# A hybrid attention step: token scales applied to x at the start, the second norm applied to the result, ReLU on ScalarE

## The chip, the cores and the metric

The kernel runs on one NeuronCore of a Trainium2 chip. The core has a matrix engine (TensorE, PE in the profile), VectorE (DVE), ScalarE (ACT), GpSimd (POOL) and SyncE (SP); here SP issues every DMA. Each engine works through its own list of instructions in order and waits at an instruction until what it needs is there. The metric is the device time of one execution in microseconds (us).

## The reference

One layer for 512 prompt tokens and 64 sample tokens (8 sequences of 8), model width 1024, all in fp32. The outputs are y for all 576 tokens, the new keys and values, and the states of the delta rule and of the convolution. What matters here:

```python
hn = rmsnorm(x, norm1_g)
proj = hn @ w_in
# mixer A: gated delta rule on qkv_a (short conv, l2norm), 4 heads of 128
oa = rmsnorm(oa, delta_norm_g) * silu(z_a)
# mixer B: dilated softmax attention, 8 heads of 64
qb = rmsnorm(q_b, q_norm_g); kb = rmsnorm(k_b, k_norm_g)
ob = dilated_attention(qb, k_all, v_all, k_past.shape[1])
h1 = x + concatenate([oa, ob]) @ w_o
hid = square(relu(rmsnorm(h1, norm2_g) @ w_up))
y = h1 + hid @ w_down
# rmsnorm(x, g) = x * rsqrt(mean(x * x) + 1e-6) * g
```

In an rmsnorm the factor of a token is one number for its whole row. It can therefore be applied before or after a product with a weight matrix, and for the squared ReLU as its square behind the MLP.

## The kernel before

**Order.** The program writes the instruction list of every engine at build time. A planner, `Flow` (lines 91 to 209), runs the pieces of the program as tasks: each task yields instructions, and the planner always takes the one that could start first by its table of costs and latencies, plus a bias by kind of task (`fl.biases`, line 1912: a task with a large bias goes behind the others). Tasks of kind "fill" are the large projections, which go where no other work for TensorE is due. The order is fixed once it is written; on the chip each engine keeps it, whatever the real durations are. Tiles come from pools with a number of slots for each use (`klass`, line 335 and on): `"q"` has 8 slots of 128x576, `"big"` 6, `"g"` (PSUM for the projections) up to 8. A task that finds no free slot stops until one is released.

**Precision.** An fp32 matrix product is three matmuls in the chip's fp32r form: high by high, high by low, low by high. So each operand is split first: ScalarE makes the high part, VectorE the rest (`wh`, `wl` for weights; `mw` holds both parts in the MLP; `xh`, `xl` for x; `xf` for the factors of the MLP's input). One matmul of a 128x128 weight block with 288 tokens is the unit of work.

**Stages.** Tokens lie along the free axis (576 of them, two halves of 288), features on partitions.

- x is loaded into `xr`, multiplied by the norm's gain g1 and split. Its mean square by token, `var1`, is taken from ScalarE's squares, GpSimd's adds and a column sum on TensorE (`ssum`). The first norm itself isn't applied to x; the stages that need it correct for it.
- proj_a (tile `pa`) makes q, k, v of the attention from the weights wq, wk, wv. proj_b (`pg<-xh`, `pg<-xl`) makes the columns of the delta mixer from wb.
- Prompt attention (`sc` scores, `e` exponentials, `ptp` their transposes, `pv`) and sample attention (`s` scores, `os` output) are laid between the matmuls of proj_b. Sample attention reads the cache in 48 loads of 512 KB, through slots `kv` and, once prompt attention has given up its memory, four more, `morekv`.
- The delta mixer: a substitution with a trip through HBM (`dl`, `dU`, loads `silvz`), triangular levels (`py`, `pt`, `pu`), and then the chain over four heads with four chunks of 128 tokens each (`cha`, `chb`; 44 matmuls in `cha`). Its sample part is `cs` and `sn`. `head_out` norms the output (`vo`, `po`).
- proj_o multiplies by w_o, first the attention half (`pg<-mob`, 192 matmuls) and then the delta half (`pg<-moa`). The first may begin when both attentions are through, and is fill beside the chain. `after_o` adds the products to the residual `h`, which `load_res` had loaded from the input.
- The MLP: z = h * g2 * S goes into quads of tiles `xq`, one quad for two feature tiles, four quads. S is a scale by token, (var1 + 1)^-1/2, taken up in `token_scale`. Two units of 128 hidden features by two (u0 and u1, "classical") use z's four parts; units u2 to u15 use a Strassen-like scheme of seven products, which also needs sums of the parts, the T sums (`t_sums`). Units of the down projection (`d`) follow. The second norm's factor R2 is known only when the squares of h are summed over all features (`square_sum`, `stats2`); it is laid out along tokens by `row_bcast` (matmuls `rowb`, copies on ScalarE).

**What the change touches.** In `x_factors` a quad takes four "q" tiles; two hold the parts of z and two the T sums. Four quads would need 16 slots, and there are 8. ReLU and R2 are applied in one VectorE pass out of PSUM, so no hidden unit can go on before R2 is there:

```python
        z = hx[i].q[2 * hf + m % 2]
        act(z, x, scale=C["g2"][:, m:m + 1])
        yield 0
        tt(z, z, st2["S"][:, c0:c1], OP.mult)
...
        yield lambda: "R2b" in done
        c0, c1 = HALF[hf]
        stt(Q[u].q[2 * hf + r], P, 0.0, st2["S"][:, c0:c1], OP.max, OP.mult)
```

Of the kernel before, what the change touches and what calls it, by code (L numbers as in the profile page):

```python
# [10 lines left out]
F32 = mybir.dt.float32  # L11
# [201 lines left out]
def hymba_step(ctx: ExitStack, tc: tile.TileContext, a):  # L213
# [106 lines left out]
    def dma(dst, src, mark=None, slow=1):  # L320
# [17 lines left out]
                      "mr": 2, "ms": 2, "mw": 6})  # L338
# [228 lines left out]

    def prep_x():
# [24 lines left out]
        rel("x", "st", "st", "big")  # L593
# [5 lines left out]
        sig("rbc")  # L599

# [172 lines left out]
    def prompt_attn():  # L773
        yield lambda: all((w, t) in done for w in "qkv" for t in range(4))
# [8 lines left out]
    def unit(u):  # L783
# [28 lines left out]
        for h in range(2):  # L812
            ts(e[h], e[h], sm[:, h, 2:3], None, OP.mult)
# [55 lines left out]
    def sample_unit(bp, qbd, sbt, sbn):  # L869
# [51 lines left out]
        ts(sm[:, 5:9], C["msel"], sm[:, 4:5], None, OP.mult)  # L921
# [230 lines left out]
    def dap(t, ap_, off=0):  # L1152
        return bass.AP(tensor=t.tensor, offset=t.offset + off, ap=ap_)

# [120 lines left out]
    def head_tokens(h):  # L1275
# [38 lines left out]
        ts(tq[:, h], ssq[:, h], 128 * EPS, 512 * EPS * EPS, OP.mult, OP.add)  # L1314
        sig(("tq", h))
# [231 lines left out]
    def head_out(c):  # L1547
# [5 lines left out]
        stt(v[:n], sso[:n, c], 1.0 / DA, tq[:n, :, c], OP.mult, OP.add)  # L1553
# [32 lines left out]
    def after_delta():  # L1586
# [4 lines left out]
        st2["acc"] = yield from get("k", [128, NT], "acc2")  # L1591
        st2["sq"] = yield from get("k", [128, 864], "sq2")
# [8 lines left out]
    def load_res():  # L1601
        yield lambda: "kv" in done
        for m in range(KT):
            x = yield from get("h1", [128, NT], "h1")
            dma(x, a["xT"][:, m], lambda t, m=m: rest.update({m: t}))
            h1[m] = x
            sig(("res", m))
            yield 0

    def after_o(m, hf, p, last):  # L1610
# [15 lines left out]
        yield 0  # L1626
        tt(z, z, st2["S"][:, c0:c1], OP.mult)
# [4 lines left out]
    def square_sum(m, hf):  # L1632
# [3 lines left out]
        if m:  # L1636
            n = 2 * m + hf
            last = [("sq", m - 1, hf)] + [("sq", (n - 3) // 2, (n - 3) % 2)] * (n >= 5)
            if not all(x in done for x in last):
                yield lambda: all(x in done for x in last)  # L1640
            n = n % 3 * 288
            s = st2["sq"][:, n:n + 288]
# [8 lines left out]
    OF_X = {1: 0, 2: 1, 3: 3, 4: 7, 5: 4, 6: 5, 7: 6}  # L1651
# [3 lines left out]
    class Quad:  # L1655
        def __init__(self, tiles):
            self.t = tiles
            self.q = [blk(tiles[j // 2], j % 2) for j in range(8)]
# [4 lines left out]
    def quad(name):  # L1663
        t = []
        for j in range(4):
# [7 lines left out]
    def t_sums(x, key):  # L1673

        q = x.q
        tt(q[4], q[2], q[0], OP.subtract)
        yield 0
        tt(q[5], q[3], q[4], OP.subtract)
        yield 0
        fl.spawn(x_parts(x, key, 4, 2), "tsum")  # L1680
        tt(q[6], q[3], q[2], OP.subtract)
        yield 0
        tt(q[7], q[1], q[5], OP.subtract)
        yield 0
        fl.spawn(x_parts(x, key, 6, 2), "tsum")
# [355 lines left out]
```

## Time and profile before

| | |
|---|---|
| median of three timed runs | 818.09 us (817.8 to 819.38) |
| the profiled execution: its own time, its span | 818.95 us, 817.2 us |
| busy in the span: TensorE, VectorE, ScalarE, GpSimd | 792.2, 568.7, 348.3, 109.4 us |
| the same as shares | 97%, 70%, 43%, 13% |
| mean DMA rate | 121 GB/s |

The profile is of one execution. Its time is 1.75 us longer than its span, which runs from the first to the last instruction. A share over the whole span hides the stages; the rows further down take it by stage. In a timeline, "[3.08 <-ACT xf L270]" says that the engine stood idle for 3.08 us before this row and that ScalarE's instruction on tile xf ended the wait.

### The profile page before, as it was taken

How to read it: one execution, taken by the hardware profiler on the slowest of the kernel's cores; microseconds unless marked ns; L12 is line 12 of the kernel's file. 1: busy time of each engine (PE TensorE's matmuls, PEld its weight loads, DVE VectorE, ACT ScalarE, POOL GpSimd, SP SyncE). 2: the span in 40 equal slices, each digit the busy share in tenths (PEclk: the TensorE clock that was granted, in tenths of full speed). 3: DMA queues.
4: the chain of work that ended last, by engine and by line, in shares of the span. 5: the costliest groups of instructions: out<-in, count | busy, mean ns of one | idle time of the engine just before them, and what ended most of it. 6: DMA issues, size and time to landing. Idle time of an engine off the chain costs nothing.

```text
span 817.2 us, 15699 instructions
## 1 busy us (share of the span) xinstructions
PE 792.2 (97%) x6323; PEld 728.1 (89%) x6323; DVE 568.7 (70%) x1250; ACT 348.3 (43%) x728; POOL 109.4 (13%) x128
## 2 busy tenths in 40 slices
PE   8989998999999999999997999999999999999998
PEld 8968877879778687778997999999999999999998
DVE  4366269888776785668798886768677676867642
ACT  5547453655242134443466543515343351534400
POOL 3443224134224000121000000000000000000000
PEclk9999999999999999999999999999999999999999
DMA  7732320106686799122221141404123130412302
GB/s 270 125 112 77 123 68 31 55 27 245 211 345 185 273 319 327 49 93 81 104 104 52 59 150 52 129 27 155 53 94 113 52 129 27 155 53 95 112 30 87
DMA packets 49864, 99.05 MB, mean 121 GB/s; under 512 B 12864, under 2 KB 26304, under 8 KB 49792
## 3 DMA queue, kind: packets, MB, share of 16 engines
q1 hardware_dynamic: 49792, 98.05, 36.6%
q8 instruction: 50, 0.82, 0.4%
q14 instruction: 22, 0.18, 0.1%
HBM read 88.15 MB, written 9.69 MB: 120 GB/s over the span
## 4 chain that ended last, share of the span: by engine, by line
PE 73%; issue 9%; DVE 7%; DMA 6%; ACT 2%; SPq 2%; POOL 1%; POOLq 0%; ACTq 0%; DVEq 0%
PE pg L262 53%; PE pa L262 7%; DVE y L285 2%; SPq L321 2%; PE cha L262 2%; DMA wr<-in_wk_dram 2%; DMA morekv<-in_cv_dram 1%; PE os L262 1%; PE ptp L265 1%; DMA morekv<-in_ck_dram 1%; PE cs L262 1%; DMA silvz<-dU 1%; PE sc L262 1%; PE s L262 1%; PE sn L262 1%
## 5 line engine op out<-in xcount | busy, mean ns | idle before, releaser
L262 PE MATMUL pg<-hid,mw 128*128 128x288 f32 x1536 | 204.7, 295 | 0.0
L262 PEld LDWEIGHTS pg<-hid,mw 128*128 128x128 f32 x1536 | 203.9, 188 | 0.0
L262 PE MATMUL pg<-xf,mw 128*128 128x288 f32 x1368 | 186.0, 297 | 4.6 <-ACT xf L270 3.8
L262 PEld LDWEIGHTS pg<-xf,mw 128*128 128x128 f32 x1368 | 183.7, 189 | 5.6 <-ACT xf L270 4.3
L278 DVE TENSOR_TENSOR h<-pg,h 128x288 f32<-128x288 f32 x160 | 72.5, 455 | 94.6 <-PE pg L262 93.8
L270 ACT ACTIVATE mw<-wr 128x512 fp32r<-128x512 f32 (+1 forms) x82 | 62.9, 791 | 70.8 <-PE pg L262 70.1
L262 PE MATMUL pg<-xh,wh 128*128 128x288 f32 x256 | 78.0, 305 | 0.0
L262 PE MATMUL pg<-xl,wh 128*128 128x288 f32 x256 | 78.0, 305 | 0.0
L262 PE MATMUL pg<-xh,wl 128*128 128x288 f32 x256 | 77.9, 304 | 0.0
L278 DVE TENSOR_TENSOR mw<-wr,mw 128x512 fp32r<-128x512 f32 (+1 forms) x82 | 72.4, 893 | 6.7 <-ACT mw L270 6.3
L270 ACT ACTIVATE mw<-ws 128x512 fp32r<-128x512 f32 x56 | 33.7, 627 | 45.3 <-PE pg L262 26.6
L262 PEld LDWEIGHTS pg<-xh,wh 128*128 128x128 f32 x256 | 48.4, 189 | 3.2 <-issue 3.0
L262 PEld LDWEIGHTS pg<-xh,wl 128*128 128x128 f32 x256 | 48.4, 189 | 2.8 <-issue 2.4
L262 PEld LDWEIGHTS pg<-xl,wh 128*128 128x128 f32 x256 | 48.5, 189 | 2.5 <-issue 1.9
L308 POOL TENSOR_TENSOR wl<-wr,wh 128x1024 fp32r<-128x1024 f32 x15 | 35.9, 2393 | 81.6 <-ACT wh L270 65.0
L262 PE MATMUL pa<-wh,xh 128*128 128x260 f32 (+1 forms) x128 | 43.1, 344 | 1.0 <-ACT wh L270 1.0
L262 PE MATMUL pa<-wh,xl 128*128 128x260 f32 (+1 forms) x128 | 43.6, 348 | 0.5 <-DVE xl L285 0.4
L262 PE MATMUL pa<-wl,xh 128*128 128x260 f32 (+1 forms) x128 | 42.7, 341 | 0.0
L270 ACT ACTIVATE wh<-wr 128x1024 fp32r<-128x1024 f32 (+1 forms) x40 | 38.6, 964 | 8.0 <-DMA wr<-in_wk_dram 5.1
L270 ACT ACTIVATE uq<-pg 128x288 f32<-128x288 f32 x42 | 17.1, 408 | 58.0 <-PE pg L262 58.0
L285 DVE SCALAR_TENSOR_TENSOR y<-u,cp,y 128x600 f32<-128x600 f32 x36 | 37.1, 1032 | 5.9 <-ACT u L270 3.3
L278 DVE TENSOR_TENSOR wl<-wr,wh 128x1024 fp32r<-128x1024 f32 (+1 forms) x25 | 28.4, 1134 | 16.0 <-ACT wh L270 15.9
(295 smaller groups left out, 1311.1 us busy)
## 6 DMA issues: line engine op xcount, KB each, us to landing
wr<-in_wu_dram SPq DMA_DIRECT2D x32, 512.0 KB, 3.3
wr<-in_wd_dram SPq DMA_DIRECT2D x32, 512.0 KB, 3.3
morekv<-in_ck_dram SPq DMA_DIRECT2D x20, 512.0 KB, 5.4
morekv<-in_cv_dram SPq DMA_DIRECT2D x20, 512.0 KB, 5.3
wr<-in_wb_dram SPq DMA_DIRECT2D x16, 512.0 KB, 4.0
wr<-in_wo_dram SPq DMA_DIRECT2D x8, 512.0 KB, 6.1
xr<-in_xT_dram SPq DMA_DIRECT2D x8, 288.0 KB, 5.6
h<-in_xT_dram SPq DMA_DIRECT2D x8, 288.0 KB, 7.2
```

The costliest lines, as they stand in the source:

```text
L262: lambda: nc.tensor.matmul(out, lhsT, rhs, start=start, stop=stop, skip_group_check=True))
L265: fl.op("PE", (97, 230), lambda: nc.tensor.transpose(out, in_, ident[:k, :k]))
L270: fl.op("ACT", cost, lambda: nc.scalar.activation(out, in_, func, bias=bias, scale=scale, accum_out=accum), mark)
L278: dve(lambda: nc.vector.tensor_tensor(out, x, y, op=op), out, x, mark=mark)
L285: dve(lambda: nc.vector.scalar_tensor_tensor(out, x, s, y, op0=op0, op1=op1), out, x, 61 if ap(s) else 0, mark=mark)
L308: fl.op("POOL", (135 + size(x) / 0.47) * slow, lambda: nc.gpsimd.tensor_tensor(out, x, y, op=op), mark)
L321: fl.op("SP", 4 * slow * size(dst) * dst.shape[0] / 360.0, lambda: nc.sync.dma_start(dst, src), mark)
```

## The change

- `scales` and `scale_x` are new: right after var1 the scale S is computed (`sc1`), laid out along tokens, and x is multiplied by it on VectorE (eight passes of 128x576). The scaled x is stored in HBM (`xsd`, eight stores), and `load_res` loads the residual from there. S also goes through HBM into `ssc`, in the layout of sample attention (one store, 16 loads). Prompt attention may begin when these loads are issued.
- Attention takes S up where e is normalised; `head_out` takes it up through `vp` and `vpa`. So all of h is scaled, and z needs no multiply by S.
- A quad takes two "q" tiles. The T sums are made in place, once the first four parts of all four quads are split.
- The second norm leaves the hidden units: ReLU is a ScalarE pass. When the token sums are there, h is multiplied by isc * R2 (`scale_h`, eight passes of 128x576), and the result by 1 / R2 just before it is stored (16 passes of 128x288). For the wait between, PSUM has 7 instead of 8 slots for "g" until R2 is laid out.
- The biases of the T sums and of the token sums (kind "acc") change, and the classical unit is written by output block.

```diff
-                      "mr": 2, "ms": 2, "mw": 6})
+                      "mr": 2, "ms": 2, "mw": 7})
...
+    def scales():
+        ts(vp, var1, 1.0, None, OP.add)
+        pow_m_half(sc1, vp, 5)
+        ts(vpa, vp, 1.0 / DA, None, OP.mult)
+        yield 0
+        recip(isc, sc1)
+        recip(es1, vp)
+        ts(es1, es1, EPS, None, OP.mult)
+
+        dma(dap(sd_, [[1, 64], [1, 1]]), sc1[:64, 4:5])
+        fl.spawn(scale_x(), "xs")
+        yield 0
+        for p in range(4):
+            for a_ in range(2):
+                for h2 in range(2):
+                    r = p * 32 + a_ * 16 + h2 * 8
+                    dma(ssc[r:r + 8], dap(sd_, [[1, 8], [16, 4]], a_ * 8))
+        yield 0
+        sig("sc")
...
+        S = yield from get("k", [128, NT], "S")
+        yield from row_bcast(S, sc1)
+        yield 0
+        for k in range(KT):
+            tt(xr[:, k], xr[:, k], S, OP.mult)
+            yield 0
+            dma(dap(xs_, [[KT * NT, 128], [1, NT]], k * NT), xr[:, k], go_on)
...
-        yield lambda: all((w, t) in done for w in "qkv" for t in range(4))
+        yield lambda: all((w, t) in done for w in "qkv" for t in range(4)) and "sc" in done
...
-            ts(e[h], e[h], sm[:, h, 2:3], None, OP.mult)
+            ts(e[h], e[h], sm[:, h, 2:3], sc1[:, i:i + 1], OP.mult, OP.mult)
...
-            dma(x, a["xT"][:, m], lambda t, m=m: rest.update({m: t}))
+            dma(x, dap(xs_, [[KT * NT, 128], [1, NT]], m * NT), lambda t, m=m: rest.update({m: t}))
...
         act(z, x, scale=C["g2"][:, m:m + 1])
-        yield 0
-        tt(z, z, st2["S"][:, c0:c1], OP.mult)
...
-        tt(q[4], q[2], q[0], OP.subtract)
...
+        tt(q[0], q[2], q[0], OP.subtract)
+        tt(q[2], q[3], q[2], OP.subtract)
+        yield 0
+        tt(q[3], q[3], q[0], OP.subtract)
+        fl.spawn(x_parts(x, key, 2, 2, 6), "tsum")
+        yield 0
+        tt(q[1], q[1], q[3], OP.subtract)
+        fl.spawn(x_parts(x, key, 0, 2, 4), "tsum")
...
-        x = hx[i] = yield from quad("xq")
+        x = hx[i] = yield from quad("xq", 2)
...
+        yield lambda: have(("x", i), range(4)) and all(have(("x", k), range(4)) for k in range(4))
         yield from t_sums(x, ("x", i))
...
-        tt(R2, R2, ims1, OP.mult)
-        pow_m_half(R2, R2, 5)
-        yield 0
-        yield from row_bcast(st2["S"], R2)
-        rel("k", "k")
+        tt(isc, isc, R2, OP.mult)
+        yield 0
+
+        yield from row_bcast(st2["acc"], isc)
+        yield 0
+        for m in range(KT):
+            fl.spawn(scale_h(m), "hsc")
+        yield lambda: all(("hs", m) in done for m in range(KT))
+        recip(R2, R2)
+        yield 0
+        yield from row_bcast(st2["acc"], R2)
...
-        yield lambda: "R2b" in done
-        c0, c1 = HALF[hf]
-        stt(Q[u].q[2 * hf + r], P, 0.0, st2["S"][:, c0:c1], OP.max, OP.mult)
+        act(Q[u].q[2 * hf + r], P, AF.Relu)
...
-        stt(q[o], q[o], 0.0, st2["S"][:, c0:c1], OP.max, OP.mult)
+        if not hf:
+            act(q[o], q[o], AF.Relu)
...
+            if hf and u >= CLASSICAL:
+                act(d, d, AF.Relu)
             act(d, d, AF.Square)
...
         if last:
+            yield 0
+            tt(h1[m][:, c0:c1], h1[m][:, c0:c1], st2["acc"][:, c0:c1], OP.mult)
             yield 0
             dma(a["yT"][:, m, c0:c1], h1[m][:, c0:c1])
...
-    fl.biases.update(tsum=1500, out=-30, acc=800, kv=1500, unit=30, conv=0, cs=30, levels=-50, attn=0)
+    fl.biases.update(tsum=300, out=-30, acc=1500, hsc=1500, xs=0, kv=1500, unit=30, conv=0, cs=30, levels=-50, attn=0)
```

The planner draws the order anew. Three places follow, each before and then after.

VectorE at the end of proj_o and the start of the MLP (xq are the quads, xf_ their split factors, one number for a quad; acc the token sums). Before:

```order
L278 TENSOR_TENSOR acc_4498<-acc_4498,sq_4499 128x288 x4
L278 TENSOR_TENSOR xf_4539<-xq,xf_4539 128x576 x2
L278 TENSOR_TENSOR xq<-xq,S 128x288 x4
L278 TENSOR_TENSOR xq<-xq 128x288
L278 TENSOR_TENSOR xf_4541<-xq,xf_4541 128x576
L278 TENSOR_TENSOR xq<-xq 128x288
L278 TENSOR_TENSOR xf_4541<-xq,xf_4541 128x576
L278 TENSOR_TENSOR xq<-xq 128x288 x2
L278 TENSOR_TENSOR acc_4498<-acc_4498,sq_4499 128x288 x4
L278 TENSOR_TENSOR xf_4540<-xq,xf_4540 128x576 x2
L278 TENSOR_TENSOR xq<-xq,S 128x288 x4
L278 TENSOR_TENSOR xq<-xq 128x288
```

After:

```order
L278 TENSOR_TENSOR h_4056<-pg,h_4056 128x288 x2
L278 TENSOR_TENSOR h_4069<-pg,h_4069 128x288 x2
L278 TENSOR_TENSOR h_4086<-pg,h_4086 128x288
L278 TENSOR_TENSOR xf_4585<-xq,xf_4585 128x576
L278 TENSOR_TENSOR h_4086<-pg,h_4086 128x288
L278 TENSOR_TENSOR xf_4585<-xq,xf_4585 128x576
L278 TENSOR_TENSOR h_4142<-pg,h_4142 128x288 x2
L278 TENSOR_TENSOR mw<-wr,mw 128x512 x3
L278 TENSOR_TENSOR xf_4586<-xq,xf_4586 128x576 x2
L278 TENSOR_TENSOR xq<-xq 128x288 x16
L278 TENSOR_TENSOR xf_4583<-xq,xf_4583 128x576 x2
L278 TENSOR_TENSOR xf_4584<-xq,xf_4584 128x576 x2
```

The multiplies by S and the adds to acc are gone from here; the T sums, before between the quads, now stand in one row of sixteen behind the last first parts.

TensorE inside the delta chain, where the first matmuls on mob stood (big_ numbers are buffers). Before:

```order
L262 MATMUL cha<-big_3441 128x128
L262 MATMUL chb<-big_3441,at 128x128
L265 MATMUL rowb<-c,sc_127 128x128 x4
L262 MATMUL cs<-so,kq 32x128 x4
L262 MATMUL pg<-mob,wh 128x288 x2
L262 MATMUL cha<-big_3442,silvz 128x128
L262 MATMUL pu<-Y,big_3442 64x64 x4
L265 MATMUL rowb<-c,sc_127 128x64
L262 MATMUL pg<-mob,wl 128x288
L262 MATMUL cha<-big_3441 128x128
L262 MATMUL chb<-big_3441,at 128x128
L262 MATMUL cha<-big_3441,silqk 128x128
```

After, at the seventh to tenth cha of the order:

```order
L262 MATMUL cha<-big_3390,silvz 128x128
L262 MATMUL os<-morekv,eTs 32x128 x4
L262 MATMUL cha<-big_3390,silvz 128x128
L262 MATMUL os<-morekv,eTs 32x128 x5
L262 MATMUL cha<-big_3389 128x128
L262 MATMUL chb<-big_3389,at 128x128
L262 MATMUL cha<-big_3389 128x128
L262 MATMUL chb<-big_3389,at 128x128
L262 MATMUL os<-morekv,eTs 32x128 x6
L262 MATMUL cha<-big_3390,silvz 128x128
L262 MATMUL os<-morekv,eTs 32x128 x3
L262 MATMUL cha<-big_3390,silvz 128x128
```

Between the steps of the chain now stand matmuls of sample attention (os); those on mob begin behind the 34th of 44 cha, before behind the fifth. The order of the changed kernel has 16 of them ahead of the last cha, before 74, and 89 matmuls of os behind the first cha, before none. (In the trace a matmul of 32x128 in fp32, as os, leaves two records.)

SP's queue at the end of the cache loads (silvz<-dU are the delta mixer's loads from HBM, wo the weights of proj_o). Before:

```order
L321 DMA silvz<-dU 128x4x128 x2
L321 DMA big_3441<-dl 128x4x128 x2
L321 DMA silvz<-dU 128x4x128 x2
L321 DMA out_conv_dram<-cv 128x324
L321 DMA morekv<-in_cv_dram 128x1024
L321 DMA wr<-in_wo_dram 128x1024 x2
L321 DMA h_3673<-in_xT_dram 128x576
```

After:

```order
L321 DMA silvz<-dU 128x4x128 x2
L321 DMA big_3389<-dl 128x4x128 x2
L321 DMA silvz<-dU 128x4x128 x2
L321 DMA out_conv_dram<-cv 128x324
L321 DMA morekv<-in_cv_dram 128x1024 x3
L321 DMA kv<-in_cv_dram 128x1024
L321 DMA morekv<-in_cv_dram 128x1024 x5
L321 DMA wr<-in_wo_dram 128x1024 x2
L321 DMA out_delta_prompt_dram<-big_3389 128x128 x2
L321 DMA h_3983<-xsd 128x576
```

One V load stood behind the last silvz load, now nine, and the weights of proj_o behind them. At the other end of the program, the store of S and one of its loads stand between the first and the second load of wv, and seven of the stores of x (with two more of those loads) between the second and the third.

## Rows read from the trace of the kernel before

**Rows 1.** Table by stage: stretch, its us, busy us by engine, clock, DMA.

```profile
core 0: us, PE busy (x) PEld busy (x) DVE busy (x) ACT busy (x) POOL busy (x), PEclk, DMA share, GB/s
0.00:100.00 100.00, 94.67 (x542) 80.98 (x543) 49.64 (x93) 55.98 (x101) 38.28 (x50) 0.98 0.49 138
...
297.00:324.30 27.30, 26.31 (x336) 21.99 (x335) 17.98 (x42) 15.54 (x61) 1.95 (x1) 1.00 0.98 330
324.30:393.10 68.80, 68.74 (x526) 55.10 (x526) 48.86 (x122) 26.23 (x90) 12.67 (x9) 1.00 0.28 95
...
418.53:443.08 24.55, 19.33 (x127) 17.94 (x125) 22.82 (x51) 16.57 (x35) 1.55 (x1) 0.93 0.12 44
443.08:813.80 370.72, 370.71 (x2795) 370.47 (x2794) 253.58 (x451) 140.89 (x235) 0.00 (x0) 1.00 0.26 86
433.90:437.50 3.60, 3.60 (x16) 3.60 (x17) 3.60 (x9) 2.85 (x7) 0.00 (x0) 0.53 0.00 0
```

**Rows 2.** PE timeline at the start of the MLP: start, us, work, idle before.

```profile
425.81 0.40 PE L262 MATMUL pg<-xf,mw 128*128 128x288 f32 x1 [0.73 <-ACT xf L270]
...
433.01 0.40 PE L262 MATMUL pg<-xf,mw 128*128 128x288 f32 x1 [3.08 <-ACT xf L270]
...
437.95 1.16 PE L262 MATMUL ssum<-c,acc 128*128 128x1 f32 x10
439.03 1.58 PE L262 MATMUL pg<-xf,mw 128*128 128x288 f32 x10
441.24 0.65 PE L265 MATMUL rowb<-c,R 128*128 128x128 f32 x4 [0.63 <-POOL R L317]
441.65 1.31 PE L262 MATMUL pg<-xf,mw 128*128 128x288 f32 x8
442.89 0.27 PE L265 MATMUL rowb<-c,R 64*128 64x64 f32 x1
```

**Rows 3.** The same stretch, instructions on tile pg alone.

```profile
418.53:443.08 24.55, 17.88 (x112) 16.31 (x110) 0.46 (x1) 0.00 (x0) 0.93 0.12 44
```

**Rows 4.** Chain of waits from 440 us to the end: start, us, what.

```profile
443.15 370.65 PE pg L262 x2794
```

**Rows 5.** DVE timeline at the start of the MLP.

```profile
431.05 1.55 DVE L278 TENSOR_TENSOR xq<-xq,S 128x288 f32<-128x288 f32 x4
```

**Rows 6.** Lines by form from 443 to 814 us: busy, mean ns of one.

```profile
L278 DVE TENSOR_TENSOR hid<-uq,hid 128x576 fp32r<-128x576 f32 x32 | 24.0, 753 | 13.2 <-ACT hid L270 13.2
...
L270 ACT ACTIVATE uq<-uq 128x576 f32<-128x576 f32 x32 | 20.4, 677 | 29.7 <-DVE uq L285 29.7
L285 DVE SCALAR_TENSOR_TENSOR uq<-uq,S 128x288 f32<-128x288 f32 x42 | 19.1, 455 | 0.9
...
L270 ACT ACTIVATE uq<-pg 128x288 f32<-128x288 f32 x42 | 17.1, 408 | 58.0 <-PE pg L262 58.0
L285 DVE SCALAR_TENSOR_TENSOR uq<-pg,S 128x288 f32<-128x288 f32 x22 | 9.8, 454 | 3.9 <-PE pg L262 3.6
```

**Rows 7.** Waits of PE: us in total, times, longest.

```profile
PE ptp L265 <- DVE e L282: 6.2, 7, 2.4
```

**Rows 8.** Timeline of all engines inside the delta chain.

```profile
339.71 0.39 PE L262 MATMUL cha<-big,silqk 128*128 128x128 f32 x2
...
344.05 0.33 DVE L285 SCALAR_TENSOR_TENSOR big<-big,eGL,cha 128x128 f32<-128x128 f32 x1
```

**Rows 9.** Stretch of the delta chain, instructions on tile mob alone.

```profile
324.30:373.00 48.70, 15.55 (x74) 10.69 (x74) 0.43 (x2) 0.43 (x2) 1.00 0.19 64
```

**Rows 10.** Stretch before it, instructions on tile os alone.

```profile
297.00:324.30 27.30, 5.07 (x112) 3.13 (x112) 1.04 (x4) 1.00 0.98 330
```

**Rows 11.** SP's queue: start and duration of DMA issues.

```profile
45.03 12.92 SPq L321 DMA_DIRECT2D wr<-in_wv_dram  x3
...
309.16 0.38 SPq L321 DMA_DIRECT2D morekv<-in_cv_dram  x1
```

**Rows 12.** VectorE timeline in proj_a: the split of the second wv tile.

```profile
70.88 1.22 DVE L278 TENSOR_TENSOR wl<-wr,wh 128x1024 fp32r<-128x1024 f32 x1
```

More of the change, by code (lines that the diff above doesn't have):

```diff
@@ L599, in prep_x @@
         sig("rbc")
+        yield from scales()
     def token_sums(src):
@@ L1590, in after_delta @@
         rel("big", "big")
-        st2["acc"] = yield from get("k", [128, NT], "acc2")
-        st2["sq"] = yield from get("k", [128, 864], "sq2")
+        x = yield from get("k", [128, 864], "acc2")
+        st2["acc"], st2["sq"] = x[:, :NT], x[:, NT:]
         cap.update(g=6, wr=3, wh=2, wl=2)
@@ L1637, in square_sum @@
             n = 2 * m + hf
[L1638 to L1642, printed above, removed]
+            last = ("sq", (n - 1) // 2, (n - 1) % 2)
+            if last not in done:
+                yield lambda: last in done
+            s = st2["sq"]
             act(s, x, AF.Square)
@@ L1657, in __init__, with quad @@
             self.t = tiles
-            self.q = [blk(tiles[j // 2], j % 2) for j in range(8)]
+            self.q = [blk(tiles[j // 2], j % 2) for j in range(2 * len(tiles))]
         def two(self, j):
             return self.t[j].rearrange("p (a t) -> p a t", a=2)
-    def quad(name):
+    def quad(name, n=4):
         t = []
-        for j in range(4):
+        for j in range(n):
             t.append((yield from get("q", [128, NT], name)))
@@ L1731, in proj_o @@
             else:
-                yield lambda: "delta" in done and "S" in done
+                yield lambda: "delta" in done
                 x = dx["moa"]
@@ L1743, in proj_o @@
         rel("big", "big")
-        cap.update(g=8, mr=4)
+        cap.update(g=7, mr=4)
         sig("proj_o")
@@ L1748, in stats2, with scale_h @@
         yield lambda: all(("sq", m, hf) in done for m in range(8) for hf in range(2))
-        yield lambda: all(("z", m, hf) in done for m in range(8) for hf in range(2))
         p = yield from token_sums(st2["acc"])
-        moment(R2, p)
+        for r0, r1, c0, c1 in ((0, 128, 0, 4), (0, 64, 4, 5)):
+            stt(R2[r0:r1, c0:c1], p[r0:r1, c0:c1], 1.0 / D, es1[r0:r1, c0:c1], OP.mult, OP.add)
         rel("x")
-        tt(R2, R2, ims1, OP.mult)
-        pow_m_half(R2, R2, 5)
+        tt(isc, isc, R2, OP.mult)
         yield 0
-        yield from row_bcast(st2["S"], R2)
-        rel("k", "k")
-        sig("R2b")
+        yield from row_bcast(st2["acc"], isc)
[6 more added lines that the diff above has]
+        yield from row_bcast(st2["acc"], R2)
+        cap["g"] = 8
+        sig("R2b")
+    def scale_h(m):
+        tt(h1[m], h1[m], st2["acc"], OP.mult)
+        mark(rest, ("h", m), 0)
+        sig(("hs", m))
+        yield 0
     hid, Q, read = {}, {}, {}
@@ L1781, in up_classical @@
         for i in range(4):
-            for hf in range(2):
-                for r in range(2):
+            for r in range(2):
+                for hf in range(2):
                     if not i:
@@ L1792, in up_classical @@
                         yield 0
-        for hf in range(2):
-            for r in range(2):
-                fl.spawn(up_relu(u, hf, r, P[hf, r]))
-        rel("mw", "mw", "mw", "mw")
+                    if i == 3:
+                        fl.spawn(up_relu(u, hf, r, P[hf, r]))
+                if i == 3:
+                    rel("mw", "mw")
     def factor(key, j):
@@ L1860, in up_square @@
     def up_square(u):
-        x = Q[u] = yield from quad("uq")
+        n = 2 if u < CLASSICAL else 3
+        x = Q[u] = yield from quad("uq", n)
         sig(("Q", u))
@@ L1876, in up_square @@
             yield 0
-        rel("q", "q", "q", "q")
+        rel(*["q"] * n)
     def add_down(m, hf, p, last):
         c0, c1 = HALF[hf]
+        key = "R2b" if last else ("hs", m)
+        if key not in done:
+            yield lambda: key in done
+        fl.at(rest["h", m][1])
         tt(h1[m][:, c0:c1], p, h1[m][:, c0:c1], OP.add)
```

58 lines of the change are left out of this document (23 added, 35 removed).

## The prediction

> **What bounds the kernel now.** I read the table by stage first. From 443 us to the end of the multiplies TensorE is busy 370.71 of 370.72 us, and in the delta chain and the projection beside it 68.74 of 68.80 us [rows 1]. There only fewer matmuls would help, and the change removes none that count (five small transposes are added). One stage is different: at the start of the MLP, 418.53 to 443.08 us, TensorE is busy 19.33 of 24.55 us, its clock is 0.93, and VectorE is the busy one with 22.82 us [rows 1]. The reader is to see there a stage in which TensorE waits for VectorE. The timeline of TensorE shows the waits: 0.73 us and 3.08 us for a factor xf, 0.63 us for GpSimd's power R before the row broadcast, and the column sums ssum in between [rows 2]. Behind the longest wait the granted clock falls to 0.53 (half speed, 1.2 GHz) for 3.6 us [rows 1]. The timeline of VectorE says why: the multiplies xq<-xq,S of the third and fourth quad come late, four of them, for one quad, only at 431.05 us [rows 5], because a quad needs four "q" tiles of eight, so quads 2 and 3 can't begin until the T sums of quads 0 and 1 are done. From 443.15 us on the chain of waits is TensorE alone, 370.65 us for 2794 matmuls, 132.66 ns each [rows 4].
>
> **The change part by part.** Start of the MLP, the term that counts. With two tiles for a quad all four fit in eight; z is one ScalarE pass without the multiply by S; the T sums stand behind the first four parts of all four quads, and the token sums far behind. The stretch holds 110 matmuls of the MLP (its weight loads on pg) [rows 3]: 110 x 0.13266 = 14.59 us. The column sums take 1.08 us (437.95 to 439.03), the five transposes 0.41 (441.24 to 441.65) and 0.26 (442.89 to 443.15) [rows 2, 4]. Together 16.34; the stretch took 24.55, so 8.21 us is loss, and I let all of it go. About 1.7 us of that is the clock (3.60 x 0.47). The stages after it are as full as before.
>
> What is late next is VectorE: its 22.82 us lose at least the eight multiplies by S (2 x 1.55) [rows 1, 5], so 19.7 us, against a need that now comes only with the first Strassen unit, after two units of 96 matmuls, 192 x 0.13266 = 25.5 us. That leaves 5.8 us of cover; if it were gone, a wait like the 3.08 us one comes back (the first rival).
>
> Added on TensorE: a second row broadcast, 0.41 + 0.26 = 0.67 us [rows 2, 4]. Both broadcasts now come in the middle of the MLP; the first waits for VectorE's R, the second for the reciprocal behind eight multiplies. In TensorE's order stand other matmuls ahead of the transposes, and all later matmuls behind. One such wait was 0.63 us with GpSimd's power in it [rows 2]; for two waits the ends are 0 and 1.26, and I take 0.63.
>
> Added at the end: the last result is multiplied before its store. By the row of a 128x288 multiply that is 0.46 us [rows 6] behind the last matmul, with nothing beside it. The sixteen store issues only move by it.
>
> VectorE and ScalarE in the MLP. Removed on VectorE: 42 and 22 passes (19.1 + 9.8 = 28.9 us) [rows 6]; added there 8 x 0.753 and 16 x 0.455 = 13.3 us; the 14 adds to the token sums only come later. ScalarE gets 22 evictions of 0.408, 14 rectifications of 128x288 (taken at 0.408 too) and 14 of 0.677: 9.0 + 5.7 + 9.5 = 24.2 us on 140.89 of 370.72, so 45% [rows 1, 6]. TensorE stands at neither, so I cost this at nothing; the cover is 370.71 us of matmuls. The evictions also free the PSUM tiles: one takes 0.408 us on ScalarE against 0.454 on VectorE [rows 6], so this does not get slower either.
> The Trainium skill speaks against this part: "ScalarE: Activation LUTs", Rules for kernel authors, wants relu and multiplies on VectorE and not on ScalarE. By that rule the passes would better have stayed where they were, and the sum would be the same or longer. The rows on evictions go the other way for fp32 out of PSUM (408 against 454 ns), so I give the rule no weight.
>
> The front. Scaling x on VectorE is 8 x 0.753 = 6.0 us (the price of a 128x576 pass) in the first 100 us, where VectorE works 49.64 [rows 1, 6]; hidden by proj_a. On SP's queue the scale's store, a scale load that waits for it and seven stores of x stand ahead of wv loads. Before, three of these were issued from 45.03 us over 12.92 us, each as a buffer came free [rows 11], and VectorE split the first of the three only at 70.88 us [rows 12]. The 25 us between are the cover; a delay beyond it would be TensorE's, us for us. The other fifteen loads stand between weight loads. The smaller steps (a second scalar in the normalisation of e, tq by vp, five 128x5 passes) lie on VectorE beside a full TensorE; at nothing.
>
> The delta chain is the open term, since the planner has drawn the front anew. Prompt attention starts later, so do the cache loads: behind the last silvz load stood one V load, at 309.16 us [rows 11], and now stand nine, with wo behind them. The 74 matmuls on mob that lay in the 48.70 us of the chain [rows 9] are now 16: 58 x 0.13266 = 7.70 us have left, to run after it. In come 89 of the small os matmuls (two records each): 178 x 5.07/112 = 8.06 us by the row of the stretch ahead [rows 10], as much as has left. If these are ready in time the chain stays covered and nothing is lost, as all is TensorE work; if they come in heaps or late and the chain keeps its 48.70 us, up to 7.70 is. The rows for the chain's own pace: one chunk takes from its first matmul at 339.71 to its state at 344.38 (344.05 and 0.33), 4.67 us, with other work in it [rows 8]; two heads at a time and sixteen chunks give 37.4 us, under the 48.70, so the chain can also close up where its cover is thin. Hence I take a value nearer to nothing, a quarter of 7.70, +1.9. Below nothing: seven waits of TensorE for e in prompt attention, 6.2 us [rows 7], could vanish, since more of proj_b now stands ahead of it. The bounds of the front are so -6.2 and +7.7.
>
> Sum, against the profiled execution's 818.95 us (span 817.2): 818.95 - 8.21 + 0.67 + 0.63 + 0.46 + 1.9 = 814.4. (The 1.75 us around the span stay.) That execution was 0.86 above the median of the runs shown, 818.09, so I say 813.5; without the chain's 1.9 it is 811.6.
>
> **The rivals.** *A, the gap comes back.* The sixteen T subtractions now stand in one row on VectorE, with their parts and the weights of u2 to split behind; the first hidden units need "q" tiles that x holds until its T sums are done, and their PSUM tiles wait for that, seven instead of eight. For it: VectorE was the busy engine here. Against: 5.8 us of cover. One wait like the longest, 3.08, with the clock behind it, 3.60 x 0.47 = 1.7: 813.5 + 4.8 = 818.3; with the wait half as long and no fall of the clock 815.
> *B, the front loses.* TensorE takes its matmuls in order, and the os now stand ahead of steps of the chain. Eight more V loads of 512 KB go after silvz; at the 330 GB/s of the stretch where the DMA is 98% busy [rows 1] that is 8 x 1.59 = 12.7 us. If the os wait for their loads, the chain waits behind them: 811.6 + 12.7 = 824.3, slower. It decides as soon as the front costs over 8.1 us (811.6 + 8.1 = 819.7). Against: cache loads were waited for little, and five slots of them are loaded ahead.
> *C, the front gains.* The waits for e go, and the chain closes up: 811.6 - 6.2 = 805.4. Against: with proj_b used early there is less of it to fill in later.
> *D, the change does what it says, and the chain takes it.* It keeps 48.70 us and the os cover none of it: 811.6 + 7.7 = 819.3, no change.
>
> **How the numbers follow.** About 0.2% (1.6 us, 816.5 to 819.7) is what a measurement of this kernel can tell from no change. The forecast has 0.55; its own range is 811 (no wait at the broadcasts, chain closed up) to 816 (half of the chain's 7.70, twice the wait). A has 0.11, a third of it faster; D 0.08; B 0.13; C 0.13. Faster: 0.55 + 0.13 + 0.04 = 0.72; the same: 0.07 + 0.08 = 0.15; slower: 0.13. The range is 806 to 820: it leaves out B and about half of C.
>
> **What would show it.** In the new profile: no wait of TensorE for xf over 1 us behind proj_o, clock 1.00 there, 192 matmuls of the first two units in 25 to 27 us (right); VectorE busy and TensorE waiting in the second unit or at the first Strassen unit (A). The table by stage over the chain: first to last cha in 49 us or less and TensorE full (forecast), TensorE under 90% with cha waiting for VectorE (D), or os waiting for DMA (B). The wait for e by total (C). A last multiply and two broadcasts with waits under 1 us. It is wrong if the time from the end of proj_b to that of proj_o grows by over 8 us, or if the first 100 us show TensorE waiting for wv.

## The result

The changed kernel takes 825.15 us (median of five runs, 823.82 to 826.72), the kernel before, timed beside it, 819.38. The ratio is 1.0073, 95% interval 1.0048 to 1.0098: slower by 0.7%, where I forecast 813.5 us. The profiled execution took 825.57 us with a span of 823.8, so against that of before (818.95) it lost 6.6 us. (The first profile of cache_loads_first, below, ran a long stretch at half clock that its timed runs don't show, so that kernel was profiled again.)

By stage, from the two profiled executions in us:

| stage | before | after | difference |
|---|---|---|---|
| to the first matmul of proj_b | 99.2 | 99.2 | 0.0 |
| from there to the first matmul of the MLP | 319.3 | 329.8 | +10.5 |
| first to last matmul of the MLP | 395.3 | 390.8 | -4.5 |
| behind the last matmul | 3.4 | 4.0 | +0.6 |

So the MLP gained, as foretold in kind, and the front lost more than that. The table by stage of the kernel after (columns as in [rows 1]):

```profile
core 0: us, PE busy (x) PEld busy (x) DVE busy (x) ACT busy (x) POOL busy (x), PEclk, DMA share, GB/s
216.00:220.00 4.00, 0.63 (x8) 0.20 (x8) 2.84 (x6) 3.62 (x8) 1.84 (x1) 0.72 0.94 350
220.00:224.00 4.00, 4.00 (x23) 3.62 (x16) 3.64 (x5) 0.18 (x1) 1.29 (x5) 0.50 1.03 415
224.00:228.00 4.00, 4.00 (x37) 3.12 (x37) 1.95 (x4) 1.48 (x2) 2.39 (x1) 0.93 1.01 342
322.40:367.60 45.20, 44.84 (x434) 32.30 (x432) 27.69 (x81) 19.29 (x74) 5.29 (x4) 1.00 0.53 186
367.60:403.60 36.00, 34.83 (x273) 28.83 (x272) 24.37 (x49) 8.52 (x18) 5.88 (x4) 1.00 0.42 145
429.01:454.50 25.49, 25.49 (x194) 25.49 (x193) 21.88 (x42) 15.84 (x32) 0.00 (x0) 1.00 0.13 42
```

The MLP's start is full now: 25.49 of 25.49 us at clock 1.00, where before it was 19.33 of 24.55 [rows 1]. The three rows from 216 us on show the new hole: TensorE works 0.63 of 4 us, and the granted clock is 0.72, then 0.50 (half speed), then 0.93. The chain (322.4 to 367.6) is shorter than before, 45.20 against 48.70 us, and what lies behind it to the end of mob is longer, 36.00 us; before it was some 20.

TensorE's waits by total name the hole (what waited, for what, us, times, longest):

```profile
PE s L262 <- DMA morekv<-in_ck_dram: 4.9, 2, 3.9
PE ptp L265 <- DVE e L282: 4.8, 6, 1.7
```

The first row was 0.8 us before. It is one matmul of the sample scores that waits 3.86 us for its cache load, and about 1 us more. SP's queue says why the load is late. After:

```profile
196.00 0.33 SPq L321 DMA_DIRECT2D kv<-in_ck_dram  x1
212.95 0.38 SPq L321 DMA_DIRECT2D dl<-E  x1
...
214.57 2.07 SPq L321 DMA_DIRECT2D morekv<-in_ck_dram  x4
```

Before:

```profile
183.23 0.38 SPq L321 DMA_DIRECT2D dl<-E  x1
...
187.63 0.33 SPq L321 DMA_DIRECT2D kv<-in_ck_dram  x1
...
193.03 2.18 SPq L321 DMA_DIRECT2D morekv<-in_ck_dram  x4
```

In both, kv is the one load that prompt attention leaves room for, and in the planner's order the four loads into morekv come when it is through (on the chip they can leave a little sooner: before, the first went out at 193.03 us and the last pv matmul ended at 196.6). After the change SP stands from 196.3 to 212.95 us at the store dl<-E of the delta mixer, whose data isn't ready, and the four loads stand behind it; before, the store was long gone.

The end of the cache loads and what lies in the chain (SP's queue, then the chain's stretch for tile mob, then for tile os):

```profile
323.88 20.26 SPq L321 DMA_DIRECT2D morekv<-in_cv_dram  x5
344.19 0.91 SPq L321 DMA_DIRECT2D wr<-in_wo_dram  x2
```

```profile
322.40:367.60 45.20, 3.59 (x16) 2.38 (x16) 0.86 (x4) 0.87 (x4) 1.00 0.53 186
```

```profile
322.40:367.60 45.20, 10.61 (x181) 5.24 (x178) 2.27 (x8) 1.00 0.53 186
```

The last V loads go out between 323.88 and 344.14 us as slots come free, the weights of proj_o at 344.19 (before 309.59), and 16 matmuls on mob lie in the chain where 74 did [rows 9].

The MLP's later waits, and the two broadcasts that the change has there (TensorE's timeline):

```profile
467.35 6.49 PE L262 MATMUL pg<-xf,mw 128*128 128x288 f32 x47 [1.17 <-DVE mw L278]
473.68 1.15 PE L262 MATMUL ssum<-c,acc 128*128 128x1 f32 x10
...
476.04 0.60 PE L265 MATMUL rowb<-c,isc 128*128 128x128 f32 x4
...
486.38 0.62 PE L265 MATMUL rowb<-c,R 128*128 128x128 f32 x4
```

No transpose waits for its broadcast (rowb); one matmul waits 1.17 us for VectorE's half of a weight, and then the column sums come. ReLU and squares on ScalarE, by form:

```profile
L270 ACT ACTIVATE uq<-uq 128x576 f32<-128x576 f32 x46 | 30.0, 680 | 1.0
...
L270 ACT ACTIVATE uq<-pg 128x288 f32<-128x288 f32 x64 | 25.9, 404 | 82.2 <-PE pg L262 82.1
...
L270 ACT ACTIVATE uq<-uq 128x288 f32<-128x288 f32 x14 | 6.0, 430 | 0.0
```

22 more evictions at 404 ns (before 408 [rows 6]) and 14 passes each of 430 and 680 ns are 24.4 us, near the 24.2 worked out.

### The profile page after: what moved, and what is told of

Same layout as the page of the kernel before. It is cut to its first block, busy times and chain, and to the rows that moved or that the text cites. A ratio compares the mean times of both kernels' runs of the same rounds, so it can differ in the third digit from the quotient of the medians.

```text
span 823.8 us, 15746 instructions
## 1 busy us (share of the span) xinstructions
PE 798.7 (97%) x6328; PEld 730.6 (89%) x6328; DVE 552.3 (67%) x1210; ACT 370.3 (45%) x780; POOL 108.5 (13%) x127
## 4 chain that ended last, share of the span: by engine, by line
PE 84%; DVE 6%; DMA 3%; ACT 2%; issue 2%; POOL 1%; SPq 0%; ACTq 0%; DVEq 0%; POOLq 0%
PE pg L262 61%; PE pa L262 7%; PE cha L262 2%; PE s L262 2%; PE os L262 2%; DMA wr<-in_wk_dram 1%; DMA morekv<-in_ck_dram 1%; DVE y L285 1%; PE cs L262 1%; PE sn L262 1%; PE ptp L265 1%; PE pv L262 1%; PE py L262 1%; PE pu L262 1%; PE chb L262 1%
## 5 line engine op out<-in xcount | busy, mean ns | idle before, releaser
L270 ACT ACTIVATE mw<-wr 128x512 fp32r<-128x512 f32 (+1 forms) x82 | 63.3, 792 | 57.1 <-PE pg L262 56.1
L270 ACT ACTIVATE uq<-pg 128x288 f32<-128x288 f32 x64 | 25.9, 404 | 82.2 <-PE pg L262 82.1
L278 DVE TENSOR_TENSOR hid<-uq,hid 128x576 fp32r<-128x576 f32 x32 | 24.1, 752 | 29.7 <-ACT hid L270 29.7
L278 DVE TENSOR_TENSOR mw<-ws,mw 128x512 fp32r<-128x512 f32 x56 | 37.2, 683 | 7.4 <-ACT mw L270 7.4
```

Source lines behind the costliest of these rows:

```text
L270: fl.op("ACT", cost, lambda: nc.scalar.activation(out, in_, func, bias=bias, scale=scale, accum_out=accum), mark)
L278: dve(lambda: nc.vector.tensor_tensor(out, x, y, op=op), out, x, mark=mark)
```

## The experiments

Two theories for the front's 10.5 us at first: (1) it is the order that the planner drew when prompt attention had to start later; (2) it is the new work itself, VectorE's eight passes and the 25 DMAs. Below, "the front" is the time from the first matmul of proj_b to the first of the MLP in a profile: 319.3 us before, 329.8 after. Ratios are to the kernel before on the same chip. In one profile the front can be a few us off by falls of the clock (token_sums_early has the very front of front_restored, and took 323.6 us against 318.8), so the ratios decide.

**front_restored.** The wait for the loads of S is taken from prompt attention:

```diff
         fl.spawn(scale_x(), "xs")
-        yield 0
+        fl.spawn(load_ssc())
+        yield 0
+
+    def load_ssc():
+        yield lambda: all((w, t) in done for w in "qkv" for t in range(4))
         for p in range(4):
...
     def prompt_attn():
-        yield lambda: all((w, t) in done for w in "qkv" for t in range(4)) and "sc" in done
+        yield lambda: all((w, t) in done for w in "qkv" for t in range(4))
```

The 16 loads are the same; they are now a task of their own.

> The changed kernel with one thing undone: prompt attention no longer waits until the 16 small loads of S are issued (they become a task of their own), so that the planner draws the front of the kernel before again (31 matmuls of proj_b ahead of the first scores instead of 97, 75 matmuls on mob ahead of the last cha instead of 16). All of the new work is kept: eight passes that scale x, the stores of x, the 16 loads. Theory 1 (the order of the front costs the 10.5 us): the MLP starts at 418 to 420 us instead of 429.0, the profiled execution takes 825.6 - 10.5 = 815.1 us, the ratio to the kernel before is 0.995 (0.992 to 0.998). Theory 2 (the new work in the front costs it, VectorE's passes and the 25 DMAs on SP's queue): the MLP starts at 427 us or later, 822 to 826 us, ratio 1.004 or more.

Measured: 818.85 us against 822.76, ratio 0.9963 (0.9937 to 0.9989). The front takes 318.8 us, the MLP 390.8, with all the new work in place. Theory 2 falls: the work is free. (The MLP starts at 422.2 us and not 418 to 420, since proj_b began 4 us late; that lies ahead of all the change does there. A weight load of proj_a landed later in most of the later profiles, and TensorE waited 2.1 us behind it.)

**before_late_attention.** One line in the kernel before:

```diff
         yield lambda: all((w, t) in done for w in "qkv" for t in range(4))
+        yield 8700
```

> The kernel before with one line added: the planner is told to start prompt attention 8.7 us later, as it starts in the changed kernel (96 matmuls of proj_b ahead of the first scores). No work is added or removed. Theory 1: the front takes some 10.5 us more, the MLP starts at 429 us with its gap of 8 us as before, 818.9 + 10.5 = 829 us, ratio 1.012 (1.009 to 1.015). Theory 2: at most 2 us more, 818 to 821 us, ratio under 1.003.

Measured: ratio 1.0189 (1.0163 to 1.0214), 833.47 us in the profiled execution, more than either theory gave; the front takes 333.7 us. With no work added, a later start alone brings the same hole: SP's queue, then TensorE's wait, then the table for 220 to 230 us:

```profile
202.45 0.33 SPq L321 DMA_DIRECT2D kv<-in_ck_dram  x1
218.39 0.38 SPq L321 DMA_DIRECT2D dl<-E  x1
...
220.01 1.98 SPq L321 DMA_DIRECT2D morekv<-in_ck_dram  x4
```

```profile
225.31 1.08 PE L262 MATMUL s<-morekv,qbd 128*32 128x256 f32 x8 [4.34 <-DMA morekv<-in_ck_dram]
```

```profile
220.00:230.00 10.00, 5.66 (x35) 4.16 (x34) 7.92 (x14) 4.52 (x10) 3.14 (x5) 0.66 0.98 351
```

SP stands at dl<-E until 218.39 us, the loads go out at 220.01, TensorE waits 4.34 us and the clock is 0.66. Theory 1 holds. That nearly the same delay cost 14 us here and 10.5 there says that the price belongs to the order drawn, not to the delay.

**What in the order costs it?** Theory K: late K loads, the wait and the clock behind it. Theory C: the chain that lost its cover of mob (the term of the prediction).

**cache_loads_first** and **cache_loads_first_again.** The changed kernel, in head_scores:

```diff
+        if h == 2:
+            yield 3000
         dma(dap(dl, [[128, 128], [129 * 128, 4], [1, 128]], h * 4 * 129 * 128), E4, "dl")
```

> The changed kernel with one line: the planner takes the store dl of the third head 3 us later, so that on SP's queue the first four cache loads into the slots morekv stand ahead of it and not behind. Prompt attention stays late (97 matmuls of proj_b ahead of it), the chain stays uncovered (89 matmuls of os behind the first cha, 10 on mob ahead of the last). Theory K (most of the front's 10.5 us is TensorE waiting for late cache loads, 4.9 us, and the clock that falls behind the wait): that wait is under 1.5 us, from the start of proj_b to the start of the MLP it takes 324 us or less (changed kernel 329.8, before 319.3). Theory C (most of it is the chain that lost its cover): the wait shrinks, but the same stretch still takes 327 us or more, since what comes earlier waits in the chain.

> The kernel of cache_loads_first once more, for a profile without the long fall of the clock that its first profile had. By its timed runs (ratio 0.9976 against 1.0073 of the changed kernel, so some 8 us) theory K expects: TensorE waits under 1.5 us for K loads, no granted clock under 0.9 between 210 and 235 us, and from the start of proj_b to the start of the MLP 320.5 to 324 us (329.8 in the changed kernel: 4.1 us of wait and 3.4 us of clock less), the chain as uncovered as there. Theory C: 327 us or more.

Measured: ratio 0.9976 (0.9947 to 1.0005), 1.0% under the changed kernel's, some 8 us. In the second profile the front takes 321.9 us, and the wait for K loads is gone. SP's queue, and the table for 210 to 230 us:

```profile
209.26 0.42 SPq L321 DMA_DIRECT2D morekv<-in_ck_dram  x1
214.69 0.38 SPq L321 DMA_DIRECT2D dl<-E  x1
```

```profile
210.00:220.00 10.00, 10.00 (x91) 8.84 (x90) 8.22 (x15) 3.36 (x6) 5.87 (x7) 1.00 0.67 223
220.00:230.00 10.00, 10.00 (x106) 8.60 (x104) 7.22 (x15) 4.70 (x9) 3.71 (x6) 1.00 0.94 358
```

One load into morekv now leaves at 209.26, ahead of dl. The other three still leave behind it, from 215.67 us on; but the redrawn order of TensorE has the first scores later too, at 218.09 us (214.87 in the changed kernel), with more of proj_b ahead of them. TensorE is full in these 20 us, at clock 1.00. The chain is as uncovered as in the changed kernel (10 matmuls on mob ahead of the last cha). So the edit gives back 7.9 of the 10.5 us by profile, and 8 by timing, with the wait for K loads gone; not all of that need be theory K's, since the order changed elsewhere too (the count further down puts some 5 there). (Of the clock I had counted too much: in the changed kernel's three rows from 216 us on TensorE idles through most of the first, so what the clock took is about 4 x 0.50 + 4 x 0.07 = 2.3 us, beside 4.1 us more of wait.)

**chain_half_covered.** The same line with `h == 3` and 5000.

> The changed kernel with one line: the planner takes the store dl of the fourth head 5 us later. Prompt attention and the first cache loads stay as late as in the changed kernel, but the end of sample attention comes earlier against the chain: 46 matmuls of os behind the first cha instead of 89, five V loads behind the last silvz load instead of nine, mob starts behind the 20th cha instead of the 34th, 28 matmuls on mob ahead of the last cha instead of 16. Theory K: from the start of proj_b to the start of the MLP 329 to 331 us, as in the changed kernel. Theory C: 327 us or less.

Measured: ratio 1.0025 (0.9996 to 1.0054), some 4 us under the changed kernel; the front takes 324.3 us. The wait for K loads is still there:

```profile
223.02 1.08 PE L262 MATMUL s<-morekv,qbd 128*32 128x256 f32 x8 [3.78 <-DMA morekv<-in_ck_dram]
```

So a part, up to 4 us, hangs on the end of sample attention too; this goes theory C's way and not theory K's, though the two intervals (that of the changed kernel begins at 1.0048) overlap a little.

**before_late_samples.** In the kernel before, `yield 12000` ahead of sample attention.

> The kernel before with one line: the planner starts sample attention 12 us later, prompt attention as before (31 matmuls of proj_b ahead of it). The cache loads come later, three V loads stand behind the last silvz load, 33 matmuls of os behind the first cha, and 51 matmuls on mob ahead of the last cha instead of 74. Theory C: the chain loses a third of its cover, from the start of proj_b to the start of the MLP 322 to 325 us (before 319.3), ratio 1.004 to 1.007. Theory K: no wait for K loads over 1.5 us, so 321 us or less, ratio under 1.002.

Measured: ratio 1.0097 (1.0072 to 1.0122), front 324.8 us. By the numbers theory C; but the trace has a wait that no other order has at this size:

```profile
214.18 0.56 PE L262 MATMUL sb<-silqk 128*64 128x64 f32 x4 [4.88 <-DVE u L278]
```

The redrawn order has the matmul on sb 4.88 us ahead of its VectorE input. Alone, this run is inconclusive on C.

**chain_uncovered.** front_restored, `yield 14000` in kv_loader ahead of the second pair's V loads.

> front_restored with one line: the planner takes the second pair's V loads 14 us later. Prompt attention, the K loads and the wait for them stay as in front_restored, and only the end of sample attention is late: 83 matmuls of os behind the first cha (0 in front_restored, 89 in the changed kernel), nine V loads behind the last silvz load, 19 matmuls on mob ahead of the last cha (75 and 16). If the uncovered chain costs about 3 us (what is left of the front's 10.5 after theory K's 7.5), the stretch from proj_b to the MLP takes 321 to 324 us (front_restored 318.8), ratio 0.999 to 1.002. If the chain's cover is the larger part (theory C): 325 us or more. If it costs nothing: 320 or less.

Measured: ratio 1.0113 (1.0039 to 1.0187), front 330.3 us. It looks like theory C at full price, but most of it lies in another place. The first matmul of proj_b to the end of mob takes 294.8 us, in front_restored 293.5. That is 1.3 more, though nine records of matmuls (four sn, four po, one cs) have moved behind it, some 2.5 us by front_restored's rows (1.12 for two sn, 0.40 for four po); so the uncovered chain cost some 4 us. The rest comes behind it. SP's queue, and TensorE's timeline:

```profile
381.71 5.78 SPq L321 DMA_DIRECT2D out_delta_sample_dram<-so  x2
387.58 0.39 SPq L321 DMA_DIRECT2D so<-in_sd_dram  x1
```

```profile
394.01 1.08 PE L262 MATMUL cs<-so,kq 128*32 128x128 f32 x32
...
399.83 2.04 PE L262 MATMUL sn<-vbd,big 64*128 64x512 f32 x2 [2.44 <-DVE vbd L278]
...
403.25 2.07 PE L262 MATMUL sn<-vbd,big 64*128 64x512 f32 x2 [0.95 <-DVE vbd L278]
405.25 0.85 PE L262 MATMUL pg<-moa,wh 128*128 128x288 f32 x2
```

The last load of the delta state (so) went out at 387.58, behind a store; the last head's cs, sn and output po follow only then, and the delta half of proj_o (moa) starts at 405.25 us, with the clock at 0.55 from 400 to 410. So an uncovered chain alone costs some 4 us here, and late loads behind it cost more.

**The parts of the front, counted.** All these kernels have the same matmuls on os, cha, chb and mob (sample attention's output, the chain, the attention half of proj_o), so the profiles can say what TensorE gives to them: the time from the start of each to the start of the next matmul, with idle time left out. Beside it stands TensorE's idle time in the front, ahead of the first cha and behind it (all in us):

| profile | front | on os, cha, chb, mob | idle ahead of the first cha | idle behind it |
|---|---|---|---|---|
| before | 319.3 | 63.4 | 11.0 | 0.1 |
| after | 329.8 | 67.4 | 13.9 | 1.5 |
| front_restored | 318.8 | 63.3 | 11.2 | 0.0 |
| before_late_attention | 333.7 | 68.6 | 14.2 | 1.1 |
| cache_loads_first_again | 321.9 | 67.4 | 10.6 | 1.3 |
| chain_half_covered | 324.3 | 63.6 | 13.4 | 0.6 |
| before_late_samples | 324.8 | 66.6 | 13.4 | 0.6 |
| chain_uncovered | 330.3 | 65.8 | 12.7 | 5.3 |

The busy time of the os alone says the same (tile os in the front; before, after, chain_half_covered):

```profile
99.20:418.53 319.33, 17.40 (x448) 11.19 (x448) 4.49 (x16) 0.99 0.48 163
```

```profile
99.20:429.01 329.81, 20.41 (x448) 11.79 (x448) 4.53 (x16) 0.98 0.47 159
```

```profile
102.80:427.10 324.30, 18.66 (x448) 11.02 (x448) 4.51 (x16) 0.98 0.48 162
```

So each theory has about half. Of the 10.5 us some 5.5 lie with the chain: the same matmuls take 4.1 us longer where they alternate, and TensorE idles 1.5 us more. The other 5 lie ahead of it: 2.9 of idle time (4.1 more of K wait, and other waits that shrank in sum), and 2.1 by which proj_b and the scores run longer, which is where the half clock behind the K wait falls. cache_loads_first leaves the chain's part as it is (67.4 and 1.3) and takes the other part away, with some 2.6 us more that the kernel before still has; chain_half_covered takes nearly all of the chain's part away (63.6 and 0.6) and leaves the K wait. In before_late_samples 3.7 of the 5.5 us lie with the chain. In chain_uncovered 1.9 of the 5.3 us of idle time lies within the chain, the rest behind mob. Each row is one profile.

**The MLP: four_tile_quads.** front_restored with `quad("xq")` of four tiles, T sums in tiles 2 and 3, and no wait for all four quads.

> front_restored with the quads of x back at four tiles (T sums in tiles of their own, so that quads 2 and 3 wait until quads 0 and 1 are through), z without the multiply by S and the late second norm kept. Theory: the tiles are what made the gap at the start of the MLP, so TensorE's waits for xf come back and the first 192 matmuls of the MLP take 29 to 33 us instead of 25.5; 3 to 8 us slower than front_restored. Rival (the multiplies by S and the early norm made it): less than 1.5 us slower.

Measured: ratio 0.9976 (0.9954 to 0.9998). The MLP takes 393.9 us, 3.1 more than in front_restored; but its first 192 matmuls take 25.6 us, as with two tiles:

```profile
421.49 34.00 PE L262 MATMUL pg<-xf,mw 128*128 128x288 f32 x254
...
474.77 0.65 PE L265 MATMUL rowb<-c,R 128*128 128x128 f32 x4 [1.90 <-DVE R L295]
```

No wait for xf of any size is back. What is lost is lost later, with VectorE busy nearly all the time (5.97 and 6.00 us of the 6 from 456 and from 468): 1.90 us at the broadcast of 1/R2, and a clock of 0.72 for the 6 us behind it. The loss is of the size that the theory gave, but not at its place; nor is it the rival's 1.5 us or less.

**token_sums_early.** front_restored with the old biases, `tsum=1500, acc=800`.

> front_restored with the old biases: T sums at 1500 instead of 300, token sums at 800 instead of 1500, so that the sums of squares come early again (114 matmuls of the MLP ahead of the column sums instead of 325). Theory (the late token sums are part of what closed the gap, since VectorE was the busy engine at the start of the MLP): the first 192 matmuls take 27 to 31 us instead of 25.6, and the MLP's multiplies 392 to 395 us instead of 390.8. Rival (the two-tile quads and the missing multiply by S do it alone): 25.6 to 27 us, and the MLP's multiplies 390 to 391 us, since the column sums cost the same anywhere and the wait of 1.2 us near the 325th matmul goes.

Measured: ratio 1.0132 (1.0098 to 1.0165), the worst of the MLP variants and far more than the theory gave: its multiplies take 403.8 us and the first 192 41.9. TensorE, VectorE and the table there:

```profile
450.21 2.28 PE L262 MATMUL ssum<-c,acc 128*128 128x1 f32 x10 [8.46 <-DVE acc L278]
```

```profile
448.73 0.46 DVE L278 TENSOR_TENSOR acc<-acc 128x288 f32<-128x288 f32 x1 [0.51 <-ACT acc L270]
449.69 0.46 DVE L278 TENSOR_TENSOR acc<-acc 128x288 f32<-128x288 f32 x1 [0.51 <-ACT acc L270]
```

```profile
440.00:450.00 10.00, 1.75 (x14) 1.52 (x12) 5.93 (x13) 4.13 (x10) 0.00 (x0) 0.70 0.19 53
450.00:460.00 10.00, 8.50 (x35) 7.87 (x36) 6.95 (x14) 4.79 (x11) 0.00 (x0) 0.50 0.00 0
```

The changed kernel keeps squares in one buffer (the kernel before had three), so a square on ScalarE and an add on VectorE alternate, 0.97 us a pair; this run is therefore no measure of what the early sums cost before. Early, TensorE stands 8.46 us at the column sums and then at a clock of 0.50. Late, the same row of pairs lies beside matmuls.

**relu_on_vectore.** front_restored with the three ReLU passes as a max on VectorE, for instance:

```diff
-        act(Q[u].q[2 * hf + r], P, AF.Relu)
+        ts(Q[u].q[2 * hf + r], P, 0.0, None, OP.max)
```

> front_restored with all ReLU passes of the MLP back on VectorE (a max with 0, 22 out of PSUM, 14 of 128x288, 14 of 128x576), the rest of the change kept. Theory: TensorE stands at neither engine in the MLP, so the time is that of front_restored within 1 us; the wait of 1.2 us for VectorE's mw near 467 us grows at most to 3 us. Rival by the rule of the Trainium skill that ReLU belongs on VectorE: faster than front_restored by 1 us or more.

Measured: 816.69 us, ratio 0.9935 (0.9912 to 0.9958), the best of all; the MLP takes 389.2 us, 1.6 less than in front_restored. TensorE's timeline there, and under it front_restored's:

```profile
422.20 46.45 PE L262 MATMUL pg<-xf,mw 128*128 128x288 f32 x348
468.49 1.29 PE L262 MATMUL ssum<-c,acc 128*128 128x1 f32 x10
```

```profile
422.22 37.16 PE L262 MATMUL pg<-xf,mw 128*128 128x288 f32 x278
460.56 6.49 PE L262 MATMUL pg<-xf,mw 128*128 128x288 f32 x47 [1.18 <-DVE mw L278]
```

The 1.18 us wait for mw is gone, and the multiplies run on to the column sums. Two of the three forms of the pass are also shorter on VectorE than on ScalarE (430 and 680 ns, above), those that don't come out of PSUM:

```profile
L282 DVE TENSOR_SCALAR uq<-pg 128x288 f32<-128x288 f32 x22 | 9.8, 455 | 5.8 <-PE pg L262 5.7
L282 DVE TENSOR_SCALAR uq<-uq 128x576 f32<-128x576 f32 x14 | 6.3, 451 | 0.0
L282 DVE TENSOR_SCALAR uq<-uq 128x288 f32<-128x288 f32 x14 | 4.2, 303 | 0.0
```

The rival was right, by the 1.6 us; the intervals of the two ratios overlap, so it rests on the profiles (the medians, 816.69 against 818.85, go the same way). This kernel beats both, by 0.65% and, against the changed kernel, by about 1.4%.

## Why the prediction was wrong

- **The start of the MLP: right, and its cause half wrong.** The 8.21 us of loss went: 192 matmuls take 25.6 us (worked out 25.5). But I put the gap on the four "q" tiles, and with four tiles the first 192 still take 25.6. With early token sums, in their one buffer and with the old bias of the T sums, the gap is back and costs 13 us. So work for VectorE and ScalarE at that place can make a gap and the tiles alone do not; which work made the old one isn't shown, since the old sums had three buffers and the multiplies by S were not tried alone.
- **Broadcasts and tail: small sizes.** No wait at the transposes (0.63 taken), 0.6 us at the tail (0.46 taken).
- **VectorE's 5.8 us of cover (rival A): nearly enough.** One wait of 1.17 us near the 325th matmul. The MLP gained 4.5 us where my terms gave 6.9 (8.21 less 0.67 and 0.63). The wait is part of what is missing; 1.05 us is spread over the last 2420 matmuls, and for that the runs give no cause.
- **ReLU on ScalarE at nothing: wrong by 1.6 us.** The row on evictions (408 against 454 ns) is right, stands for 22 of the 50 passes only, and was no answer: ScalarE also makes the high half of each weight, VectorE's half follows on it, and TensorE waited for that. The Trainium skill, "ScalarE: Activation LUTs", Rules for kernel authors, puts relu on VectorE; the run agrees in the outcome, with 389.2 against 390.8 us.
- **The front: the step that failed.** The prediction named the delta chain "the open term" and took +1.9 us within -6.2 and +7.7; it was +10.5. I followed SP's queue past the loads of wv, where nothing came of it (99.2 us to proj_b in both), and at its far end behind silvz, but not at the first loads into morekv. In the planner's order these come at the end of prompt attention, which moved from 196.6 to 208.3 us (its last pv matmul), and the new order has dl<-E ahead of them. That kv, dl and morekv are close neighbours there the queue's rows of before show (183.23 to 193.03 us, above); they belonged among the rows I read. TensorE's wait for these loads and the half clock behind it have no term in the sum; by the count above they make some 5 of the 10.5 us. The other part is the chain, 1.9 taken and some 5.5 found. It did close up, from 48.4 to 45.0 us between its first and last cha, as the 4.67 us of a chunk said. But I took the os that came in at the price of the stretch ahead, 8.06 us for 178 records; they took 10.61 for 181 (above), and the cha themselves, start to start, 13.4 instead of 11.3 us. Why the same matmuls take longer where they alternate, no run shows.
- **Rival B came nearest in time (824.3), for a neighbouring reason:** cache loads late on SP's queue and TensorE in order behind them, but K loads at 215 us, not V loads in the chain. I gave it 0.13.
- **C:** the waits for e went from 6.2 to 4.8 us only.

## What to carry to other kernels

Where a planner writes the order, a new condition on an early stage is a change of every stage behind it: list what that stage releases (here the memory for the next loads), and follow each in the queue that issues it, up to the instruction that stands ahead of it. A queue that issues all DMAs in order makes a store whose data is late into a wait for every load behind it; and the holes of 3 to 4 us in TensorE's work seen here (3.08 before, 3.86 after) had a stretch at half clock behind them, worth some 2 us more. Matmuls that are laid singly between the steps of a chain are not to be priced as in a row. For a gap at a stage's start, first move out the sums that are needed late.

## What the runs showed that I had not expected

Moving one store by 3 us in the plan was worth 8 us on the chip, and a planned delay of 8.7 us cost 14. Small changes of the order bring waits of 2 to 9 us at places that no term names (s 3.86, sb 4.88, ssum 8.46 us), and the granted clock fell behind or in most of the holes: 0.50 over 10 us in token_sums_early, 0.55 in chain_uncovered, 0.66 in before_late_attention.
